# The order of the experts in a streamed mixture of experts: those of several items moved one distance forward

## The chip, the cores and the metric

The kernel runs on one core of one Trainium2 chip. The metric is device microseconds of one execution of the whole kernel. Three runs of the kernel before took 1101.43, 1099.33 and 1100.4 us; their median is 1100.4 us.

## The reference

One decoder layer is computed for 512 prompt tokens and for 32 sample tokens (8 sequences of 4): an input projection, an mLSTM branch and a sliding-window attention branch, their merge, a layer norm, a hierarchical mixture of experts with its layer norm, and a gated embedding with the last layer norm. The change lies in the mixture of experts alone:

```python
N_GROUPS, EXPERTS_PER_GROUP, TOP_K = 4, 8, 2        # 32 experts, D_MODEL 1024, D_EXPERT 512
def hier_moe(x, w_rg, b_rg, w_re, b_re, w_eg, w_eu, w_ed):
    g_idx = jnp.argmax(g_logits, axis=-1)                   # one group of experts for a token
    top_p, top_i = lax.top_k(softmax(e_logits_of_group), TOP_K)
    gate = g_w * top_p / top_p.sum(-1, keepdims=True)
    ...
def expert_block(args):
    h = jax.nn.silu(xblk @ w_gate[e]) * (xblk @ w_up[e])
    return h @ w_down[e]                                    # times gate, added to the token's row
```

Each of the 544 tokens goes to two experts. The sum over a token's two experts doesn't depend on the order in which the experts are worked off.

## The kernel before

**Items, places and slots.** After the router, the rows of each expert are cut into items of up to 32 rows. An expert has a place in a list; the program walks the list and, at each place, does all items of that expert. An expert's weights are 6 MB: gate and up in two halves of 2 MB each (tiles `w`, `w2a`, `w2b`, `gu3a`, `gu3b`) and down in two halves of 1 MB (`w`, `w2c`, `w2d`, `r_p`). There is room for four experts, slots 0 to 3 (NB = 4). Slots 0 and 1 have the tile name `w`, slot 2 has `w2a`, `w2b`, `w2c`, `w2d`, slot 3 has `gu3a`, `gu3b` and `r_p`. Place p uses slot p modulo 4, but the last places are put on the last slots: with 26 places, places 24 and 25 lie in slots 2 and 3, and so place 24 takes over the slot of place 22, and place 25 that of place 23 (the number `gap`, L219 to L225 and L395 to L412).

**The guess.** Four experts are fetched before the router has answered (L1749, `prefetch`). They are ranks 16 to 19 by the biases, and they stand at places 0 to 3 whatever the router says (`firsts`, L1808).

**The order of the others** is made by sorting keys on DVE (L2041 to L2080). An expert of one item (`kinds[:, 0]`) has the key n - 0.5, where n is its running number among those of one item, `nth[:, 0]`. An expert of several items (`kinds[:, 1]`) has the key n * ratio, where n is its running number among those of several, `nth[:, 1]`, and ratio is the number of those of one item divided by the number of those of several plus one (L2046 to L2050). `ties` adds a little for equal keys and puts the four fetched ahead in front; `base` adds 1000 where an expert has no item. So those of several items are spread evenly over those of one.

**The loads.** SP issues all weight loads in the order of the places (`load_place`, L199). Each load of place p waits for the place that had the slot before: for the first half of gate and up, until PE has done that half for its last item (semaphore `gh`), for the second half `gu`, and for the down weights `dn`, the last down product (L203 and L206). SP issues in order, so a load that waits holds back all loads behind it. Behind the last place's loads SP issues the `late` loads (L227): the rows x1 (2 MB) and the first half of `w_pg` (2 MB, semaphore `al`), which go into slot 0 and which the tail of the kernel needs.

**The work on an item.** PE does gate and up for the item (64 matmuls at L306 in the trace, 32 for each half), and then the down product of the item before (32 matmuls at L318 in the trace), since ACT (L440) and DVE (L515, L479) need time to turn gate and up into the hidden rows. DVE scales the product (L486) and POOL scatters it into `ybuf` (L265). Every fourth item PE transposes the next 128 rows (L298). The last item's down product stands at L415, its scaling at L533, its scatter at L286.

**The end of the stage.** It is one critical block: SP leaves it when all scatters have landed (L237 to L239) and ACT has finished (`fin`); ACT's last wait is for `al`, the landing of `w_pg` (L465). Only then does the tail begin (L2371 and on).

Of the kernel before, what the change touches and what calls it, by code (L numbers as in the profile page):

```python
# [15 lines left out]
ALU = mybir.AluOpType  # L16
# [528 lines left out]
def tile_decoder_step(ctx: ExitStack, tc: tile.TileContext, *aps):  # L545
    nc = tc.nc
    A = dict(zip(_INS + _CONSTS + _OUT_NAMES, aps))
    sy, act, dve, pe, gp = nc.sync, nc.scalar, nc.vector, nc.tensor, nc.gpsimd
# [125 lines left out]
    for pp in range(2):  # L674
        gp.dma_start(
            out=brow[16 + 4 * pp:20 + 4 * pp, :].rearrange("j (a d) -> j a d", a=2),
# [1260 lines left out]
    with ExitStack() as scope:  # L1937
# [26 lines left out]
        def rt(name, shape, dt=F32):  # L1964
            n = -(-count(shape) // 8) * 8
            if dt != F32 or taken[0] + n > arena.shape[1]:
                return R.tile(shape, dt, name=name)
            taken[0] += n
            return view(arena[:, taken[0] - n:taken[0] - n + count(shape)], shape)
# [21 lines left out]
        items, flag, base, key = (rt(n, [P, NEXP]) for n in ("items", "flag", "base", "key"))  # L1991
# [43 lines left out]
        kinds, nth = rt("kinds", [P, 2, NEXP]), rt("nth", [P, 2, NEXP])  # L2035
        ratio = rt("ratio", [P, 1])
# [12 lines left out]
        dve.scalar_tensor_tensor(out=key, in0=nth[:, 0], scalar=-0.5, in1=kinds[:, 0], op0=ALU.add, op1=ALU.mult)  # L2049
        dve.tensor_tensor(out=ratio, in0=ratio, in1=nth[:, 0, NEXP - 1:], op=ALU.mult)  # L2050
        dve.tensor_tensor(out=base, in0=base, in1=key, op=ALU.add)
        dve.scalar_tensor_tensor(out=key, in0=nth[:, 1], scalar=ratio, in1=kinds[:, 1], op0=ALU.mult, op1=ALU.mult)
        dve.tensor_tensor(out=key, in0=key, in1=base, op=ALU.add)

        E = NEXP
        sq, kcol, bcol_ = rt("sq", [E, E]), rt("kcol", [E, 1]), rt("bcol", [E, 1])
# [36 lines left out]
        for n, by, op, m_ in ((80, K["turns"][0:1], ALU.add, 16), (82, iota[0:1, 0:32], ALU.mult, 32)):  # L2093
# [4 lines left out]
                                 op0=ALU.mult, op1=ALU.subtract)  # L2098
# [10 lines left out]
                          in1=hi[:, :, None].to_broadcast([P, 2 * NT5, 20]), op=ALU.is_equal)  # L2109
# [357 lines left out]
```

## Time and profile before

| quantity | value |
|---|---|
| median of the runs | 1100.4 us |
| the profiled execution | 1102.54 us |
| its span, first to last instruction | 1100.6 us |
| PE busy | 1003.2 us (91%) |
| DVE busy | 512.0 us (47%) |
| ACT busy | 369.0 us (34%) |
| POOL busy | 255.7 us (23%) |
| bytes moved by DMA | 256.45 MB, 233 GB/s on the mean |

The busy shares are means over stages of different kinds. The stage of the experts runs from 646.84 us, PE's first matmul of place 0, to 1019.06 us, PE's first matmul of the tail. In the timeline PE's runs of matmuls at L306 carry the tile names of the slots, which gives the number of items at each place: 26 places with 49 items. Places 0 to 3 have one item each. The other 22 places, 4 to 25, have

1, 1, **2**, 1, **3**, 1, 1, **8**, 1, **3**, 1, 1, **3**, 1, **5**, 1, 1, **5**, 1, **2**, 1, 1

items: 14 places of one item, and 8 places of several (2, 3, 8, 3, 3, 5, 5, 2 in their order). All 26 experts are read once.

### The profile page before, as it was taken

What the parts mean: (1) busy time and instruction counts of PE and PEld (TensorE: products, weight loads), DVE (VectorE), ACT (ScalarE), POOL (GpSimd) and SP (SyncE); (2) the same over time, 40 slices, a digit from 0 to 9 for tenths busy, and PEclk for the clock granted to TensorE, in tenths of its full rate; (3) what the DMA queues carried; (4) which work ended last, traced back from release to release, by engine and by line L of the source; (5) the groups of instructions that cost most, each with busy time, mean ns of one, the idle gap of its engine ahead of it and who ended that gap; (6) DMA issues with size and microseconds to landing.
All of it is one profiled execution on the core that took longest, in us unless ns stands there. A gap on an engine that the chain in (4) does not pass through costs nothing.

```text
span 1100.6 us, 26984 instructions
## 1 busy us (share of the span) xinstructions
PE 1003.2 (91%) x10269; PEld 823.1 (75%) x10270; DVE 512.0 (47%) x1308; ACT 369.0 (34%) x751; POOL 255.7 (23%) x385
## 2 busy tenths in 40 slices
PE   9999999999999998999999976875988888986987
PEld 8988999999988886899989634553556565654775
DVE  5555533645767765565566731111122222222696
ACT  5311224533677776523321311110111111223531
POOL 6000000501355555312410211111222222221011
PEclk9999999999999998999999988999899999999699
DMA  8321322222515423534379889999999999979701
GB/s 257 78 78 54 101 77 77 67 68 85 159 46 184 156 97 122 183 93 137 109 278 407 339 307 393 426 427 426 426 427 426 427 426 427 426 319 400 291 34 63
DMA packets 90892, 256.45 MB, mean 233 GB/s; under 512 B 11115, under 2 KB 58433, under 8 KB 70820
## 3 DMA queue, kind: packets, MB, share of 16 engines
q1 hardware_dynamic: 76036, 224.61, 52.9%
q0 software_dynamic: 10272, 27.21, 7.0%
q10 hardware_dynamic: 4512, 3.64, 1.1%
q8 instruction: 49, 0.80, 0.3%
q14 instruction: 23, 0.19, 0.1%
HBM read 241.89 MB, written 19.61 MB: 238 GB/s over the span
## 4 chain that ended last, share of the span: by engine, by line
PE 77%; DMA 7%; issue 6%; SPq 4%; DVE 4%; ACT 1%; POOL 1%; DVEq 0%; ACTq 0%; POOLq 0%
PE pj L709 14%; PE pj L710 14%; PE pj L711 13%; PE psG L306 13%; PE kept L318 6%; SPq L137 3%; DMA gu3b<-in_w_eu_dram 2%; DMA w<-in_w_pg_dram 2%; SPq L143 1%; PE sp L1397 1%; PE psX L298 1%; PE nm L1385 1%; PE sp L767 1%; DMA wg_in<-in_w_in_dram 1%; PE pp L2267 1%
## 5 line engine op out<-in xcount | busy, mean ns | idle before, releaser
L709 PE MATMUL pj<-xH,wH 128*128 128x256 f32 (+1 forms) x672 | 197.4, 294 | 0.0
L710 PE MATMUL pj<-xL,wH 128*128 128x256 f32 (+1 forms) x672 | 196.1, 292 | 0.0
L711 PE MATMUL pj<-xH,wL 128*128 128x256 f32 (+1 forms) x672 | 194.7, 290 | 0.0
L592 ACT CAST wH<-raw 128x1024 fp32r<-128x1024 f32 x76 | 79.6, 1048 | 200.5 <-PE pj L710 127.1
L709 PEld LDWEIGHTS pj<-xH,wH 128*128 128x128 f32 x672 | 126.5, 188 | 4.6 <-issue 3.7
L710 PEld LDWEIGHTS pj<-xL,wH 128*128 128x128 f32 x672 | 126.4, 188 | 2.2 <-issue 1.6
L711 PEld LDWEIGHTS pj<-xH,wL 128*128 128x128 f32 x672 | 126.2, 188 | 2.1 <-issue 1.9
L593 DVE TENSOR_TENSOR wL<-raw,wH 128x1024 fp32r<-128x1024 f32 x76 | 95.4, 1256 | 64.7 <-ACT wH L592 64.5
L474 DVE COPY xT<-xg 128x256 f32 x48 | 14.4, 299 | 224.6 <-PE psG L306 224.6
L306 PE MATMUL psG<-w,xT 128*32 128x256 f32 x1408 | 87.0, 401 | 28.6 <-issue 23.2
L306 PEld LDWEIGHTS psG<-w,xT 128*32 128x32 f32 x1408 | 53.6, 115 | 60.0 <-issue 39.0
L440 ACT ACTIVATE both<-psG 128x128 f32<-128x128 f32 x49 | 13.6, 278 | 242.9 <-PE psG L306 242.9
L1373 POOL TENSOR_SCALAR lg<-lg,sm 128x256 f32<-128x256 f32 (+1 forms) x64 | 59.0, 934 | 44.9 <-DVE sm L1370 34.7
L265 POOL DMA_INDIRECT ybuf<-ysb,idy x48 | 47.6, 991 | 43.6 <-POOL idy L262 39.6
L426 ACT ACTIVATE xg<-psX,gcol 128x128 f32 (+1 forms) x100 | 36.3, 467 | 51.4 <-PE psX L298 51.4
L709 PE MATMUL pj<-wH,xH 128*128 128x256 f32 x160 | 46.8, 292 | 1.0 <-DVE vs L923 1.0
L318 PE MATMUL kept<-w,hT 128*32 128x256 f32 x704 | 44.2, 390 | 2.5 <-DVE hT L479 2.5
L710 PE MATMUL pj<-wL,xH 128*128 128x256 f32 x160 | 44.4, 277 | 0.0
L711 PE MATMUL pj<-wH,xL 128*128 128x256 f32 x160 | 44.3, 277 | 0.0
L306 PE MATMUL psG<-gu3a,xT 128*32 128x256 f32 x480 | 30.7, 398 | 14.7 <-issue 6.7
L479 DVE STREAM_TRANSPOSE hT<-both 128x128 f32<-128x128 f32 x49 | 20.1, 409 | 45.4 <-PE kept L318 45.0
L306 PE MATMUL psG<-w2a,xT 128*32 128x256 f32 x384 | 26.6, 423 | 15.9 <-issue 12.8
(655 smaller groups left out, 2281.4 us busy)
## 6 DMA issues: line engine op xcount, KB each, us to landing
w<-in_w_eg_dram SPq DMA_DIRECT2D x24, 1024.0 KB, 24.9
w<-in_w_eu_dram SPq DMA_DIRECT2D x24, 1024.0 KB, 27.2
w<-in_w_ed_dram SPq DMA_DIRECT2D x24, 1024.0 KB, 27.4
raw<-in_w_in_dram SPq DMA_DIRECT2D x22, 1024.0 KB
r_p<-in_w_ed_dram SPq DMA_DIRECT2D x14, 1024.0 KB, 24.5
w2a<-in_w_eg_dram SPq DMA_DIRECT2D x7, 1024.0 KB, 20.0
w2a<-in_w_eu_dram SPq DMA_DIRECT2D x7, 1024.0 KB, 22.4
w2b<-in_w_eg_dram SPq DMA_DIRECT2D x7, 1024.0 KB, 23.6
```

Source lines behind the costliest of these rows:

```text
L137: return [eng.dma_start(out=W[s][half][:, i], in_=w[i][bass.ds(e, 1)].rearrange("a (p k) f -> (a p) k f", p=P)[:, ks]) for i in range(2)]
L265: gp.indirect_dma_start(out=ybuf.rearrange("t (q d) -> (t q) d", q=4), out_offset=bass.IndirectOffsetOnAxis(ap=idy[:, r:r + 1], axis=0), i ...
L306: m = pe.matmul(psG[32 * q:32 * q + 32], xT[:, k], W[s][half][:, :, kh, P * q:P * q + P], start=k == 0, stop=k == KD - 1)
L318: m = pe.matmul(out[32 * q:32 * q + 32], hT[:, 32 * k:32 * k + 32], W[s][2][k // 2][:, k % 2, 256 * q:256 * q + 256], start=k == 0, stop=k ...
L426: m = act.activation(out=out, in_=psX[:, k], func=AF.Identity, bias=gcol[:, 1, k:k + 1], scale=gcol[:, 0, k:k + 1])
L479: dve.transpose(out=hT[:].rearrange("p (r t) -> p r t", r=4), in_=h[:].rearrange("p (f r) -> p r f", r=4)).then_inc(S["ch"], 1)
L592: act.copy(out=H, in_=src)
L593: return eng.tensor_tensor(out=L, in0=src, in1=H.bitcast(F32), op=ALU.subtract)
L709: pe.matmul(out, lh(k), rh(k), start=start and i == 0, stop=False)
L710: pe.matmul(out, lh(k), rl(k), start=False, stop=False)
L711: pe.matmul(out, ll(k), rh(k), start=False, stop=stop and i == len(ks) - 1)
L1373: gp.tensor_scalar(out=lg[:, par, j, 0:nk], in0=lg[:, par, j, 0:nk], scalar1=sm[:, 2, par, j:j + 1], scalar2=None, op0=ALU.mult)
```

## The change

Two DVE instructions that make the keys of the experts of several items:

```diff
-        dve.scalar_tensor_tensor(out=key, in0=nth[:, 1], scalar=ratio, in1=kinds[:, 1], op0=ALU.mult, op1=ALU.mult)
-        dve.tensor_tensor(out=key, in0=key, in1=base, op=ALU.add)
+        dve.scalar_tensor_tensor(out=key, in0=nth[:, 1], scalar=-1.0, in1=kinds[:, 1], op0=ALU.add, op1=ALU.mult)
+        dve.scalar_tensor_tensor(out=key, in0=key, scalar=ratio, in1=base, op0=ALU.mult, op1=ALU.add)
```

The key n * ratio becomes (n - 1) * ratio. The keys of the experts of one item, of the four fetched ahead and of those without items stay. With 14 of one item and 8 of several the ratio is 14/9 = 1.556: the keys of those of several were 1.556, 3.111, ... 12.444, and become 0, 1.556, ... 10.889, between those of one item at 0.5, 1.5, ... 13.5. Places 4 to 25 then have

**2**, 1, 1, **3**, 1, **8**, 1, 1, **3**, 1, **3**, 1, 1, **5**, 1, **5**, 1, 1, **2**, 1, 1, 1

items. The expert of eight items goes from place 11 to place 9, the last one of several (2 items) from place 23 to place 22. Slots, waits, the loads' order by place and the `late` loads are as before.

## Prediction

> **What bounds the kernel now.** I read the span first, then the windows over the stage of the experts, then PE's and SP's timelines there, and at last the chain that ended last. The first line is the page's span; the profiled execution took 1102.54 us, 1.94 above it and 2.1 above the runs' median of 1100.4. The sum below is made on this trace and carried to the median as a difference.
>
> ```profile
> span 1100.6 us, 26984 instructions
> ```
>
> The windows (length, busy PE, PEld, DVE, ACT, POOL, PEclk, DMA share, GB/s) show DMA at its ceiling for most of the stage, and one hole:
>
> ```profile
> 810.00:830.00 20.00, 16.14 (x293) 10.90 (x289) 4.25 (x13) 2.12 (x4) 3.64 (x7) 1.00 1.01 425
> 930.00:950.00 20.00, 16.98 (x264) 11.61 (x268) 2.78 (x8) 4.73 (x11) 4.79 (x8) 0.91 1.01 426
> ...
> 966.00:968.00 2.00, 2.00 (x44) 1.23 (x40) 0.00 (x0) 1.67 (x5) 1.02 (x2) 1.00 0.74 301
> 968.00:970.00 2.00, 1.83 (x36) 0.83 (x28) 0.52 (x3) 1.07 (x2) 1.22 (x2) 1.00 0.21 78
> 970.00:972.00 2.00, 0.60 (x12) 0.50 (x16) 0.85 (x2) 0.49 (x1) 1.17 (x2) 1.00 0.16 66
> 972.00:974.00 2.00, 2.00 (x44) 1.43 (x37) 0.00 (x0) 0.00 (x0) 0.98 (x1) 1.00 0.16 66
> 974.00:976.00 2.00, 2.00 (x44) 1.47 (x40) 0.49 (x2) 0.28 (x1) 0.00 (x0) 1.00 0.91 246
> ```
>
> Against 426 GB/s the five rows miss 125 + 348 + 360 + 360 + 180 = 1373, times 2 us, over 426: **6.45 us** of transfer are lost. SP's queue says why:
>
> ```profile
> 818.94 0.33 SPq L137 DMA_DIRECT2D gu3a<-in_w_eg_dram  x1
> ...
> 939.12 4.27 SPq L143 DMA_DIRECT2D r_p<-in_w_ed_dram  x2
> 973.53 0.34 SPq L137 DMA_DIRECT2D w2a<-in_w_eg_dram  x1
> ```
>
> Place 23's last load is issued at 939.12, place 24's first only at 973.53: slot 2 is still held by place 22. PE comes to place 22 late:
>
> ```profile
> 728.89 1.93 PE L306 MATMUL psG<-w,xT 128*32 128x256 f32 x32 [1.29 <-DMA w<-in_w_eu_dram]
> ...
> 747.10 3.66 PE L306 MATMUL psG<-w,xT 128*32 128x256 f32 x64 [2.03 <-issue]
> ...
> 760.50 1.93 PE L306 MATMUL psG<-w2b,xT 128*32 128x256 f32 x32 [1.39 <-DMA w2b<-in_w_eu_dram]
> ...
> 770.45 3.64 PE L306 MATMUL psG<-gu3a,xT 128*32 128x256 f32 x32 [6.29 <-DMA gu3a<-in_w_eu_dram]
> 775.20 3.64 PE L306 MATMUL psG<-gu3b,xT 128*32 128x256 f32 x32 [1.11 <-DMA gu3b<-in_w_eu_dram]
> 778.61 1.43 PE L318 MATMUL kept<-w2c,hT 128*32 128x256 f32 x16
> ...
> 787.66 1.93 PE L306 MATMUL psG<-gu3a,xT 128*32 128x256 f32 x32 [0.35 <-issue]
> ...
> 793.36 1.93 PE L306 MATMUL psG<-gu3a,xT 128*32 128x256 f32 x32 [0.31 <-issue]
> ...
> 851.16 1.93 PE L306 MATMUL psG<-w2a,xT 128*32 128x256 f32 x32 [1.52 <-issue]
> ...
> 858.06 1.93 PE L306 MATMUL psG<-gu3a,xT 128*32 128x256 f32 x32 [0.42 <-issue]
> ...
> 866.60 3.66 PE L306 MATMUL psG<-w,xT 128*32 128x256 f32 x64 [3.15 <-issue]
> ```
>
> Those are halves of the places 8, 9, 10, 11 (eight items), 14, 15 and 16. Up to place 11, PE waits for DMA. From 775.20 it has work without a break, since place 11 alone takes some 45 us, in which DMA fills the other slots. So PE is the late one from 775.20 to the hole. The next lines are place 22, place 23's two items and place 25's two halves:
>
> ```profile
> 971.40 1.93 PE L306 MATMUL psG<-w2a,xT 128*32 128x256 f32 x32 [1.56 <-issue]
> ...
> 978.04 1.93 PE L306 MATMUL psG<-gu3a,xT 128*32 128x256 f32 x32 [1.26 <-issue]
> ...
> 983.59 1.93 PE L306 MATMUL psG<-gu3a,xT 128*32 128x256 f32 x32 [0.16 <-issue]
> ...
> 999.60 1.93 PE L306 MATMUL psG<-gu3a,xT 128*32 128x256 f32 x32 [1.79 <-DVE both L515]
> 1002.21 1.93 PE L306 MATMUL psG<-gu3b,xT 128*32 128x256 f32 x32 [0.68 <-DMA gu3b<-in_w_eu_dram]
> ```
>
> Behind the hole DMA is the bound again: PE waits for place 25's gu3b, and the chain goes from SP's last issue through the landing of w_pg straight to the tail:
>
> ```profile
> 996.36 22.29 DMA w<-in_w_pg_dram
> 1018.65 0.02 issue
> ...
> 1019.06 3.75 PE po L150 x16
> ```
>
> So bytes that are late at 967 are late at 1018.65. All bytes are the same in both orders; only the hole can change.
>
> **The change, part by part.** *The two instructions.*
>
> ```profile
> L2052 DVE SCALAR_TENSOR_TENSOR xg<-nth,ratio,kinds x1: 253/253/253, 628.9 to 628.9; 128x32 f32<-128x32 f32 x1
> L2053 DVE TENSOR_TENSOR xg<-xg x1: 192/192/192, 629.2 to 629.2; 128x32 f32<-128x32 f32 x1
> ```
>
> The second becomes a scalar_tensor_tensor like the first, 192 to 253 ns: +0.06 us on the router's chain, counted in full (bounds 0 and +0.1).
>
> *Where PE's unbroken run begins.* The eight items now stand at place 9, slot 1. Places 4 to 8 hold eight items in five places in both orders (1, 1, 2, 1, 3 before; 2, 1, 1, 3, 1 after), so PE is through with them no later than before, at 747.10. The weights of place 9: the second halves of places 8 and 10 landed at 728.89 and 760.50, the middle is 744.7; by the step from place 10 to 11 (14.7) it is 745.8. I take 745, bounds 744.7 and 747.1. The run begins 30 us earlier.
>
> *When it reaches place 22.* Before, 971.40 - 775.20 = 196.2 us for 30 items at 11 places. After, there lie 32 items at 13 places between: two places of one item more. Such a place takes 858.06 - 851.16 = 6.9 us or 978.04 - 971.40 = 6.6 us, and 866.60 - 858.06 = 8.5 us where the loop turns over (bound). The same three turns and the same eight transposes lie between as before. 745 + 196.2 + 13.5 = 954.7; upper bound 747.1 + 196.2 + 17 = 960.3.
>
> *Place 24's first load.* Place 22 now has two items. The second follows the first by 793.36 - 787.66 = 5.7 us, its first half takes 1.93, SP issues 0.2 later (973.53 after 971.40 + 1.93): 962.5, bounds 962.2 and 968.1. It is needed before DMA runs dry. The 966 row's 301 GB/s put the last byte at 967.4; the 974 row's 246 puts the first new byte at 974.85, 1.3 after the issue. The deadline is 966.1: 3.6 us to spare, at the upper bound 2.0 us of hole.
>
> *What is late next.* SP then waits for place 22's last down product, behind place 23's gate and up: place 23 begins at 954.7 + 5.7 + 6.6 = 967.0, gate and up 3.66, down 1.9, so 972.6; place 24's gate and up, 4.19 MB at 426, keep DMA until 967.4 + 9.85 = 977.2. Place 25's loads queue behind and are not late either. The other new risk is place 13, which follows the eight items in slot 1 as place 15 did in slot 3. Place 15's load was issued 818.94 - 775.20 = 43.7 us after the run's begin, and the 810 row (425 GB/s) shows no hole there. Place 13's comes at 745 + 43.7 = 788.7; DMA has work to 745 + 4.9 (place 9's down, 2.1 MB at 426) + 3 x 15.8 (three places, each half of 760.50 - 728.89) = 797.3, so the deadline is 796.0.
>
> *The end.* w_pg lands 6.45 us earlier, at 1012.2. Beside it runs the last scatter:
>
> ```profile
> 1011.29 1.13 POOL L286 DMA_INDIRECT ybuf<-both,idy  x1 [1.90 <-DVE both L533]
> ...
> DMA to landing us min/median/max: 5.8/5.8/6.0
> ```
>
> It lands at 1011.29 + 5.8 = 1017.1, 14.9 after place 25's gu3b at 1002.21. That weight also lands 6.45 earlier, at 995.75, so the scatter at 1010.65 if PE runs as before. But PE will have had nothing to do for some 10 us between places 24 and 25: it is through with place 24's gate and up 3.66 after 977.2, and place 25's first half lands 4.9 before 995.75. After its 6.29 us of idleness at 770.45 both halves took 3.64 instead of 1.93, and the next sixteen matmuls 1.43: on place 25's second half that is 1.7, and some 0.4 behind it. The scatter lands at 1012.7, and now ends last, 0.5 behind w_pg.
>
> By the Trainium skill, "TensorE: Matmul & The Clock Gate", Part 1, an idle window of about 3.4 us halves PE's clock and as long a busy stretch restores it, and its advice to leave no such gaps speaks against singles at the end. By it, place 25's chain would lose half of 3.4, 1.7 us, and the stage would end at 1012.35. The trace agrees only roughly: 3.15 us idle before 866.60 left the 64 matmuls at 3.66.
>
> *The sum.* -6.45 (hole) + 0.5 (cold chain behind it) + 0.06 (key) = **-5.9 us**: the median goes to 1100.4 - 5.9 = 1094.5, the profiled execution to about 1096.6, its span to 1094.7.
>
> **The rivals.**
>
> *A: part of the hole stays*: PE comes to place 22 by 5 to 7.3 us later than summed (the upper bounds of its start and of the singles together are 5.6), which leaves a hole of 1.4 to 3.7: 1095.9 to 1098.2. For it: the margin of 3.6 us rests on a run of 210 us. Against: that run is a measured one plus two singles.
>
> *B: PE stays cold through the whole last chain*: gate, down, spread, down each lose about 1.7 (3.64 against 1.93 for 32 matmuls), 6.8 in all; the scatter lands at 1010.65 + 6.8 = 1017.5 and the gain is 1.15: 1099.3. For it: the stage's last three places are now single, with PE mostly idle. Against: at 778.61 PE was nearly warm again after 3.6 us. Here belongs, too, that the order comes out as before or that the hole was never on the path (1100.4); the keys and the chain speak against it.
>
> *C, slower: a hole behind the eight items.* Place: place 13's load. If PE's run at place 9 began x us after 745, for x over 7.3 there is a hole of x - 7.3 there, and the old hole at place 24 comes back with 3.7 besides (x - 3.6 less the first hole's x - 7.3). It decides from x = 12.3 on, where both exceed 6.45 by 2.2 us. At x = 15 it is 7.7 + 3.7 - 6.45 = 4.95: 1105.4. For it: three items at place 7 and eight at place 9 stand close together. Against: PE has done as many items by then as before, and was at place 9 at 747.10 then, and it had 6.29 us idle before place 11.
>
> **How the numbers follow.** Forecast 68%, A 13%, B and no change 12%, C 7%. Within 0.2%, 2.2 us, is about what a measurement of this kernel can't tell from no change (the runs lie 2.1 apart). Faster: 68 + 13 = 81%; same 12%; slower 7%. The predicted time is the likeliest case's, 1094.5, whose own range is 1092.9 (the whole hole gone, no cold chain, 1.05 of spread below) to 1096. Up to 1098.2 with A it holds 81%; I take B's 1099.3 in as the upper end, since the cold chain's length is the term with the fewest rows behind it.
>
> **What would show it.** In the windows: no row under 400 GB/s between 690 and 1005; in SP's queue, place 24's first w2a issue at 962 or before, with DMA still at 426; the eight items' run from about 745 to 790 in slot 1 (`w`), place 13's load at about 789; PE waiting for DMA at place 24 and at place 25; w_pg landing near 1012, the last scatter near it, the tail's first matmul near 1013; the tail itself, 81.5 us, unchanged. Wrong it would be if the hole stands at another place, if PE waits for nothing before place 24, or if the stage's end moves earlier and the tail grows.

## The result, and the profile after

The kernel after took 1093.27 us at the median (1091.31 to 1094.4, four runs), beside 1100.49 (1099.33 to 1101.43, four runs) for the kernel before on the same chip: a ratio of 0.993 [0.9906, 0.9955]. The forecast was 1094.5, faster, with 1092.9 to 1099.3 around it. The ratio puts 1100.4 at 1092.7 [1090.1, 1095.4]: the sign is right, the gain is 7.2 us by the medians where 5.9 were forecast, and the middle of the measurement lies 0.2 us under the low end. Two single executions of before, at 1417.9 and 1482.18 us, stand far outside all others and are left out of all that follows.

The profiled execution of after took 1093.82 us, 8.72 less than the 1102.54 of before. First its span:

```profile
span 1091.9 us, 26980 instructions
```

The windows of 2 us at the old hole, and one behind it (columns as before: busy PE, PEld, DVE, ACT, POOL, PEclk, DMA share, GB/s):

```profile
966.00:968.00 2.00, 2.00 (x44) 1.47 (x40) 0.38 (x1) 0.00 (x0) 0.56 (x2) 1.00 0.98 414
968.00:970.00 2.00, 2.00 (x44) 1.44 (x39) 0.49 (x2) 0.28 (x1) 0.61 (x1) 1.00 0.97 356
970.00:972.00 2.00, 0.66 (x15) 0.16 (x4) 0.88 (x2) 0.00 (x0) 0.00 (x0) 1.00 0.98 414
...
980.00:982.00 2.00, 1.45 (x28) 0.73 (x20) 0.00 (x0) 1.69 (x5) 0.91 (x1) 1.00 1.01 352
```

Where 78 and 66 GB/s stood, the lowest row has 356; behind it, the rows from 978 to 984 have 387, 352 and 360. DMA's share is 0.96 to 1.01 in all of these, so its engines had work and moved less. SP's queue in after: place 13's load, place 23's last, place 24's first, and w_pg:

```profile
789.54 0.33 SPq L137 DMA_DIRECT2D w<-in_w_eg_dram  x1
...
950.77 0.81 SPq L143 DMA_DIRECT2D r_p<-in_w_ed_dram  x2
967.41 0.34 SPq L137 DMA_DIRECT2D w2a<-in_w_eg_dram  x1
...
988.23 2.11 SPq L230 DMA_DIRECT2D w<-in_w_pg_dram  x1
```

Place 24's load goes out 6.1 us earlier than the 973.53 of before. PE's timeline has the eight items from 744.53, place 22 at 959.73, place 24 at 982.35, place 25's two halves, and the tail's first four groups:

```profile
744.53 5.35 PE L306 MATMUL psG<-w,xT 128*32 128x256 f32 x64 [2.17 <-issue]
...
809.57 5.35 PE L306 MATMUL psG<-w,xT 128*32 128x256 f32 x64 [3.08 <-issue]
...
865.37 5.27 PE L306 MATMUL psG<-w,xT 128*32 128x256 f32 x64 [3.12 <-issue]
...
943.65 5.35 PE L306 MATMUL psG<-w,xT 128*32 128x256 f32 x64 [3.19 <-issue]
...
959.73 1.93 PE L306 MATMUL psG<-w2a,xT 128*32 128x256 f32 x32 [1.39 <-issue]
...
982.35 1.93 PE L306 MATMUL psG<-w2a,xT 128*32 128x256 f32 x32 [0.90 <-issue]
...
992.89 3.64 PE L306 MATMUL psG<-gu3a,xT 128*32 128x256 f32 x32 [6.88 <-DMA gu3a<-in_w_eu_dram]
997.92 3.64 PE L306 MATMUL psG<-gu3b,xT 128*32 128x256 f32 x32 [1.39 <-DMA gu3b<-in_w_eu_dram]
...
1014.36 3.75 PE L150 MATMUL po<-gb,keep 48*128 48x128 f32 x16 [3.21 <-SPq L179]
1018.04 4.51 PE L2267 MATMUL pp<-keep 128*128 128x256 f32 x10
1022.48 2.05 PE L150 MATMUL po<-gb,keep 48*128 48x128 f32 x16
1024.45 1.99 PE L2267 MATMUL pp<-keep 128*128 128x256 f32 x8
```

The chain that ended last goes through place 25's second half and the last scatter, no longer through w_pg:

```profile
981.22 16.66 DMA gu3b<-in_w_eu_dram
997.92 3.64 PE psG L306 x32
...
1008.98 4.72 DMA ybuf<-both,idy
```

The stage ends 1019.06 - 1014.36 = 4.70 us earlier. The span is 8.7 shorter, so 4.0 came out of the tail (from PE's first matmul behind the stage to the end of the span), which the change doesn't touch. The same groups of before's tail show where:

```profile
1022.74 4.63 PE L2267 MATMUL pp<-keep 128*128 128x256 f32 x10
1027.31 3.78 PE L150 MATMUL po<-gb,keep 48*128 48x128 f32 x16
1031.02 3.78 PE L2267 MATMUL pp<-keep 128*128 128x256 f32 x8
```

The granted clock in before's windows there (PEclk, the third number from the end) is half to 1034, as in this row:

```profile
1029.00:1034.00 5.00, 5.00 (x17) 4.24 (x17) 1.52 (x3) 1.17 (x2) 0.00 (x0) 0.50 1.03 420
```

A spread (L150) is a group of matmuls of 48 rows by 128 columns, and its product (L2267) is the group behind it. The second spread and its product took 3.78 and 3.78 in before, and 2.05 and 1.99 in after: PE ran at half its clock for about 15 us at the tail's begin in the one profile, for about 8 us in the other. The four groups together are 3.6 of the 4.0 us. So two questions went to the chip: does the stage's gain come from the hole at place 24, and is the tail's part the change's work or chance?

### The profile page after: what moved, and what is told of

Read it like the earlier page. It is cut to its first block, busy times and chain, and to the rows that moved or that the text cites. A ratio compares the mean times of both kernels' runs of the same rounds, so it can differ in the third digit from the quotient of the medians.

```text
span 1091.9 us, 26980 instructions
## 1 busy us (share of the span) xinstructions
PE 1000.6 (92%) x10269; PEld 821.9 (75%) x10270; DVE 512.2 (47%) x1308; ACT 368.9 (34%) x751; POOL 255.8 (23%) x385
## 3 DMA queue, kind: packets, MB, share of 16 engines
q10 hardware_dynamic: 4512, 3.64, 1.1%
## 4 chain that ended last, share of the span: by engine, by line
PE 82%; issue 7%; DMA 5%; DVE 4%; ACT 1%; SPq 0%; POOL 0%; DVEq 0%; ACTq 0%; POOLq 0%
PE psG L306 17%; PE pj L709 14%; PE pj L710 14%; PE pj L711 14%; PE kept L318 7%; DMA gu3b<-in_w_eu_dram 2%; PE sp L1397 1%; PE psX L298 1%; PE nm L1385 1%; PE sp L767 1%; DMA w<-ybuf 1%; DMA wg_in<-in_w_in_dram 1%; PE po L711 1%; PE tp L1352 1%; PE tp L1350 1%
## 5 line engine op out<-in xcount | busy, mean ns | idle before, releaser
L306 PE MATMUL psG<-w,xT 128*32 128x256 f32 x1664 | 105.1, 408 | 28.6 <-issue 27.6
L306 PEld LDWEIGHTS psG<-w,xT 128*32 128x32 f32 x1664 | 64.0, 117 | 67.0 <-issue 44.6
L318 PE MATMUL kept<-w,hT 128*32 128x256 f32 x832 | 51.9, 388 | 2.5 <-DVE hT L479 2.5
L318 PEld LDWEIGHTS kept<-w,hT 128*32 128x32 f32 x832 | 31.9, 112 | 16.8 <-DVE hT L479 2.8
L306 PE MATMUL psG<-gu3a,xT 128*32 128x256 f32 x416 | 26.8, 400 | 15.4 <-issue 8.5
```

Source lines behind the costliest of these rows:

```text
L306: m = pe.matmul(psG[32 * q:32 * q + 32], xT[:, k], W[s][half][:, :, kh, P * q:P * q + P], start=k == 0, stop=k == KD - 1)
L318: m = pe.matmul(out[32 * q:32 * q + 32], hT[:, 32 * k:32 * k + 32], W[s][2][k // 2][:, k % 2, 256 * q:256 * q + 256], start=k == 0, stop=k ...
```

## The experiments

Theories for the stage. **T1**, the prediction's: the time lies in the hole, which goes because PE's long run begins earlier and so place 22 is done, and place 24 loaded, earlier. **T2**: the gain comes from the end of the order, where the last places are now single items and little work is left for PE behind the last bytes. For the tail: either the length of PE's idle time ahead of it sets how long it runs cold (theory C), or it is chance, and differs between executions of one kernel.

All kernels keep the computation; where matmuls are added, their results are not used. Each ratio is to runs of before on the same chip.

**Front alone.** All experts of several items but the last move forward; the last stays where it was in before. From place 4 on: 2, 1, 1, 3, 1, 8, 1, 1, 3, 1, 3, 1, 1, 5, 1, 5, 1, 1, 1, 2, 1, 1 items. Against after:

```diff
-        dve.scalar_tensor_tensor(out=key, in0=nth[:, 1], scalar=-1.0, in1=kinds[:, 1], op0=ALU.add, op1=ALU.mult)
+        dve.scalar_tensor_tensor(out=flag, in0=nth[:, 1], scalar=nth[:, 1, NEXP - 1:], in1=nth[:, 1], op0=ALU.is_ge, op1=ALU.add)
+        dve.scalar_tensor_tensor(out=key, in0=flag, scalar=-1.0, in1=kinds[:, 1], op0=ALU.add, op1=ALU.mult)
```

> The seven other experts of several items move one distance forward, the last one (2 items) stays at place 23. Theory 1 (the unbroken run of PE begins earlier, so place 22 is done before DMA runs dry): place 22 is a single, place 24's first load is issued 5.6 us before the changed kernel's 967.4, near 962; no hole; the stage ends as in the changed kernel, the tail's first matmul near 1014; about 1093. Theory 2 (the gain comes from what stands last, three singles instead of a pair and two singles): as before, 1100.5, with a hole of about 6 us.

Measured: 1092.38 us (1089.99 to 1094.94), ratio 0.9922 [0.9896, 0.9949]. Place 24's first load and the tail's begin in its profile:

```profile
961.34 0.34 SPq L137 DMA_DIRECT2D w2a<-in_w_eg_dram  x1
...
1013.44 3.75 PE L150 MATMUL po<-gb,keep 48*128 48x128 f32 x16 [2.96 <-SPq L179]
```

The whole gain is there with before's end of the order (place 23 with two items). T2 falls.

**End alone.** Only the last of several moves, against before; places 4 to 20 stay, the last have 5, 2, 1, 1, 1:

```diff
-        dve.scalar_tensor_tensor(out=key, in0=nth[:, 1], scalar=ratio, in1=kinds[:, 1], op0=ALU.mult, op1=ALU.mult)
-        dve.tensor_tensor(out=key, in0=key, in1=base, op=ALU.add)
+        dve.scalar_tensor_tensor(out=flag, in0=nth[:, 1], scalar=nth[:, 1, NEXP - 1:], in1=nth[:, 1], op0=ALU.is_ge, op1=ALU.subtract)
+        dve.scalar_tensor_tensor(out=key, in0=flag, scalar=ratio, in1=kinds[:, 1], op0=ALU.mult, op1=ALU.mult)
+        dve.tensor_tensor(out=key, in0=base, in1=key, op=ALU.subtract)
```

> Only the last expert of several items moves, from place 23 to 22; the eight items stay at place 11. Theory 1: place 24's first load waits for place 22's second item, 973.5 + 5.6 = 979.1; the hole grows from 6.45 to about 12 us and the time by 5.6, to 1106. Theory 2: the last three places are single as in the changed kernel, so most of the stage's gain is there: about 1095.

Measured: 1107.61 us (1106.05 to 1112.02), ratio 1.0058 [1.0029, 1.0086]. Place 22 has two items now and is no earlier, so the slot is held longer:

```profile
981.05 1.93 PE L306 MATMUL psG<-w2a,xT 128*32 128x256 f32 x32 [0.16 <-issue]
```

```profile
970.00:972.00 2.00, 2.00 (x44) 1.17 (x36) 0.00 (x0) 1.78 (x6) 1.12 (x2) 1.00 0.43 158
972.00:974.00 2.00, 1.93 (x36) 0.91 (x28) 0.49 (x2) 0.97 (x2) 1.22 (x2) 1.00 0.06 16
...
980.00:982.00 2.00, 1.84 (x39) 1.06 (x32) 0.75 (x2) 0.00 (x0) 0.00 (x0) 1.00 0.00 0
```

The first row is the first half of place 22's second item at 981.05; place 24's load followed at 983.18. The rows below are windows in the hole, which is about twice as long. Half of the change by itself makes the kernel slower: with two items place 22 holds its slot for longer, and nothing ahead of it has moved forward to make up for that. (In this profile the whole stage also begins 2.2 us later than in the mean of before's, at 649.32, which is part of its late end.)

**Half the distance, and half a distance too late.** In after's line the constant -1.0 becomes -0.5 (the eight items at place 10), or +1.0 (the eight at place 12, five at place 22, two at the last place):

```diff
-        dve.scalar_tensor_tensor(out=key, in0=nth[:, 1], scalar=-1.0, in1=kinds[:, 1], op0=ALU.add, op1=ALU.mult)
+        dve.scalar_tensor_tensor(out=key, in0=nth[:, 1], scalar=-0.5, in1=kinds[:, 1], op0=ALU.add, op1=ALU.mult)
```

> Half a distance forward: eight items at place 10, pair still at place 23. Theory 1: the run begins 14.7 us earlier than before and has one single (6.7 us) more to do, place 22 begins about 963.4 to 967, place 24's first load 965.5 to 969: a hole of 0 to 3 us, the tail's first matmul near 1014 to 1016. Theory 2: as before, hole about 6 us, 1019.

> One distance backward: eight items at place 12, five items at place 22, the pair last. Theory 1: the run begins 15.8 us later than before, place 22's fifth item is at about 980, place 24's first load at about 982: a hole of about 15 us, and two items instead of one behind the last weights, 5.6 us more: about 1114. Theory 2: only the pair at the end counts: about 1106.

Measured: half the distance 1092.57 us (1091.09 to 1096.9), ratio 0.9935 [0.9908, 0.9962], place 24's load at 965.35; later 1107.61 us (1104.41 to 1112.03), ratio 1.0069 [1.0036, 1.0102], place 24's load at 977.73. The order can be moved both ways, and the time follows the hole at place 24's load. (End alone and the later order come to the same time although their loads went out 5 us apart: DMA ran dry at about 969 in the one and at about 965 in the other.) Once the load is early enough, nothing more is won: half the distance gives what the whole one gives. The later order was expected at 1114 and came to 1107.61. Its load went out at 977.73 and not at 982, and the hole cost 13.4 us and not 15; that is a part of the 6 us, and the rest isn't split up.

**The two kernels again, unchanged**, for the tail and for the spread:

> The kernel before, unchanged: a second profile of its tail. Theory C (the clock at the tail's start follows from how long PE sat idle ahead of it, 5.5 us before and 3.2 us after): the tail takes 81.5 us again, with PE at half clock for some 15 us. Theory P (it is chance where the clock's window falls): the tail may as well take 77.5 us, with half clock for some 8 us.

> The changed kernel, unchanged. Theory C: the tail takes 77.5 us again. Theory P: it may take 77 to 82 us.

> The kernel before, a third profile. What is open is how often its tail takes 81.5 us (first profile) or 76.8 (second). If the long tail is chance (theory P): the stage ends at 1017 to 1019 with a hole of 6.5 to 7 us, and the tail takes 76.5 to 78 or about 81.5. If the order before brings it about: about 81.5 in most profiles.

> As the third: hole 6.5 to 7 us, stage's end 1017 to 1019, tail either 76.5 to 78 or about 81.5.

> The changed kernel, a third profile. Theory P: no hole over 2 us, the stage ends at 1013 to 1014.5, and the tail may be long (about 81.5) here as well as short. If the order decides: short.

Measured: before 1096.63 us (1092.01 to 1101.8, ten runs; ratio to the other runs of before there 0.9986 [0.9962, 1.001]), after 1093.49 us (1088.82 to 1094.96, eleven runs), ratio 0.995 [0.993, 0.997]. Three more profiled executions, one each, took 1099.32 and 1099.25 us for before and 1092.76 for after. The tail in the second profile of before:

```profile
1017.44 3.75 PE L150 MATMUL po<-gb,keep 48*128 48x128 f32 x16 [5.80 <-SPq L179]
1021.12 3.75 PE L2267 MATMUL pp<-keep 128*128 128x256 f32 x10
1024.79 2.05 PE L150 MATMUL po<-gb,keep 48*128 48x128 f32 x16
1026.77 1.99 PE L2267 MATMUL pp<-keep 128*128 128x256 f32 x8
```

5.80 us of idle time ahead, the longest of all profiles, and a short tail: theory C falls. Before's long tail was one of four, and none of the nine other profiles in the table has one. All profiles together (loss: the shortfall of the 2 us windows from 960 to 1000 against 426 GB/s, as time; stage end: PE's first matmul of the tail; tail: the span less that):

| kernel | span | place 24's load | loss | stage end | tail |
|---|---|---|---|---|---|
| before | 1100.6 | 973.53 | 6.96 | 1019.06 | 81.5 |
| before, second | 1094.2 | 972.18 | 6.89 | 1017.44 | 76.8 |
| before, third | 1097.4 | 973.62 | 7.72 | 1019.21 | 78.2 |
| before, fourth | 1097.3 | 974.38 | 9.06 | 1019.65 | 77.7 |
| after | 1091.9 | 967.41 | 1.44 | 1014.36 | 77.5 |
| after, second | 1091.6 | 963.82 | 0.26 | 1013.51 | 78.1 |
| after, third | 1090.9 | 966.98 | 1.33 | 1012.66 | 78.2 |
| front alone | 1091.1 | 961.34 | 0.24 | 1013.44 | 77.7 |
| end alone | 1104.9 | 983.18 | 14.06 | 1028.22 | 76.7 |
| half the distance | 1090.7 | 965.35 | 0.62 | 1012.81 | 77.9 |
| later | 1104.9 | 977.73 | 13.39 | 1027.97 | 76.9 |
| before, filled | 1095.8 | 971.83 | 7.67 | 1019.41 | 76.4 |
| after, filled | 1091.0 | 966.45 | 1.93 | 1014.58 | 76.4 |

Means of the four of before and the three of after: loss 7.66 and 1.01 (-6.65), stage end 1018.84 and 1013.51 (-5.33), tail 78.5 and 78.0 (-0.6, from the unrounded values), span 1097.4 and 1091.5 (**-5.9**). The stage begins between 646.3 and 648.0 in all rows but end alone; at the mean it begins 0.5 us later in after than in before.

**Matmuls put ahead of the tail.** Behind PE's last wait of the stage, eight products of 128 by 256 in before, four in after (16 and 8 in the trace), to keep PE warm:

```diff
         pe.wait_ge(S["sc"], len(halves))
+        for _ in range(8):
+            pe.matmul(wide[0][:, 0:256], ident, any_, start=True, stop=True)
```

> The order before, with 8 matmuls more on PE (128x256 f32, results unused) between the last copies of the stage and its end, so that PE isn't idle there. The stage ends as before, 1019. If the slow clock at the tail's start is what the tail's 4 us hang on, it starts warm: the tail takes 77.5 us or less and the time is 1096.5. If the tail's 4 us hang on something else (when DMA brings ybuf's rows, say), it stays 81.5 and 1100.5.

> The changed order, with 4 such matmuls at the same place. In the changed kernel's profile PE was done with the tail's first matmuls before the rows were normalised, so a warm start is worth at most 1 us there: 1092 to 1093.3; where a run of the changed kernel has the long cold tail, up to 4 us.

Measured: before filled 1100.83 us (1095.28 to 1103.45), ratio 1.002 [0.9997, 1.0043]; after filled 1093.64 us (1090.27 to 1095.22), ratio 0.9955 [0.9937, 0.9973], no better than after beside it. In before's:

```profile
1012.35 6.74 PE L419 MATMUL psX<-keep 128*128 128x256 f32 x16 [0.68 <-ACT r_p L457]
...
1019.41 2.02 PE L150 MATMUL po<-gb,keep 48*128 48x128 f32 x16 [0.32 <-SPq L179]
```

The added matmuls ran cold themselves, 6.74 us for 16, but behind them the tail's first spread took 2.02 instead of 3.75. The tail is 76.4 in both, about 2 less than the 78.5 and 78.0 of the means. The timed runs show none of these 2 us in either kernel; where they go in the executions without a profile stays open.

**A warm last chain.** Eleven products ahead of place 25's items, in the loop over the slots:

```diff
+                if s == NB - 1:
+                    with pe.If(a + 1 > full):
+                        pe.wait_ge(S["c4"], ng)
+                        for _ in range(11):
+                            pe.matmul(wide[0][:, 0:256], ident, any_, start=True, stop=True)
```

> The changed order, with 11 matmuls more on PE (128x256 f32, results unused) between place 24's and place 25's gate and up, so that PE is not idle there. If the cold chain behind place 25's weights sets the stage's end: both halves of place 25 take 1.93 instead of 3.64, the last scatter lands 1.5 to 2 us earlier, and the stage ends where w_pg lands, 0.3 to 0.7 us earlier than in the first profile of the changed kernel. If the cold chain is hidden: no change within 0.2 us.

Measured: 1191.84 us (1187.81 to 1194.5), ratio 1.0847 [1.0825, 1.0868]. The edit changed something else as well. PE's groups behind a turn of its loop over the places, here the first of them, and the chain's rows:

```profile
704.76 6.19 PE L306 MATMUL psG<-w,xT 128*32 128x256 f32 x64 [17.79 <-issue]
```

```profile
846.37 18.42 issue
...
1018.55 13.78 issue
```

The same turn in after:

```profile
687.75 5.34 PE L306 MATMUL psG<-w,xT 128*32 128x256 f32 x64 [3.55 <-issue]
```

What DMA carried for instructions in the stage (packets, MB, share), first this kernel's from 650 to 1110, then after's from 650 to 1010:

```profile
q8 instruction: 53, 0.87, 0.8%
```

```profile
q8 instruction: 6, 0.10, 0.1%
```

47 more packets of instructions, and 13.8 to 18.4 us without work ahead of the first group behind each of the five turns instead of 2.4 to 3.6. Together that is 81 us instead of 15, some 66 of the 98 us that this kernel is slower than after; the rest isn't split up. The rows speak for PE's loop being fetched again at each turn once its body is that little longer. That is argued from the rows, not tried by itself. On the cold chain the run says nothing; the profiles of after answer that, below.

## Where the prediction was right, and which step failed

**The mechanism in the stage is shown.** The hole at place 24 was worth nearly what the stage's end moved: 6.65 us of loss went, the stage ended 5.33 earlier and had begun 0.5 later, and the cold chain at the end, below, took some tenths back. Front alone takes the hole away and keeps the gain (loss 0.24, 1092.38 us), end alone doubles it and is slower by about 6.4 us (0.0058 of 1100.8), and in the table the kernels with a loss of 13 to 14 end the stage at 1028, those with 7 to 9 at 1017 to 1020, those under 2 at 1013 to 1015. The forecast's -5.9 is the difference of the mean spans. That the figures are equal is luck in part, since the spans of before's four profiles lie 6.4 apart. The runs agree in kind: 72 of before (1092.0 to 1105.7) have the median 1098.8, 16 of after (1088.8 to 1095.0) have 1093.1. But these are mixed from several chips. On the chip of the first runs the medians differ by 7.2 us; on the chip of the repeats, with 43 and 11 runs, by 3.9 (the means by 5.4). So the gain is sure, and its size is known to about 2 us.

**Where the run begins** was right: 744.53 against 745. **When it reaches place 22** was not: 959.73 against 954.7, 5.0 later, under the bound of 960.3. The run takes 215.2 us instead of the 209.7 summed. Four groups of 64 matmuls in after took 5.3 us instead of 3.66, at the run's begin and behind 3.1 to 3.2 us of idle time where the loop turns over: 1.7 each. Before's run held two such losses, the second half at 775.20 and one turn:

```profile
931.83 5.35 PE L306 MATMUL psG<-w,xT 128*32 128x256 f32 x64 [3.11 <-issue]
```

Two more make 3.4 of the 5.5; the other 2.1 lie within the bounds of the two singles (13.5 to 17). The second profile of after begins warm, has two cold groups (at 808.22 and 940.06), and comes to place 22 that much earlier:

```profile
744.96 3.66 PE L306 MATMUL psG<-w,xT 128*32 128x256 f32 x64 [1.96 <-issue]
...
940.06 5.35 PE L306 MATMUL psG<-w,xT 128*32 128x256 f32 x64 [3.25 <-issue]
...
956.10 1.93 PE L306 MATMUL psG<-w2a,xT 128*32 128x256 f32 x32 [1.38 <-issue]
```

**Place 24's first load** therefore came at 967.41, not 962.5, past the deadline of 966.1, and some loss stayed: 1.44, against 0.26 in the second profile. Only 0.44 of it stands at the old hole (the rows from 966 to 972), and 0.84 from 978 to 984; since DMA's share is near 1 in these rows, they speak for slower transfers rather than missing work, and why they are slower isn't shown. So the condition of rival A (5 us late) just came true, but not its price: a hole of 1.4 at place 24 didn't come. The prediction's "no row under 400 GB/s" failed with 356 and 352. And one of its signs of being wrong appeared: PE did not wait for DMA ahead of place 24 in this profile (0.90 on issue), since it came there late itself. In the second profile, with two cold groups less, it did wait, for place 24's second half:

```profile
982.62 1.93 PE L306 MATMUL psG<-w2b,xT 128*32 128x256 f32 x32 [1.83 <-DMA w2b<-in_w_eu_dram]
```

**What is late next** was right. Place 13's load went out at 789.54 (forecast 788.7), and no hole came:

```profile
790.00:810.00 20.00, 13.96 (x253) 9.05 (x249) 4.13 (x12) 2.71 (x6) 4.60 (x8) 1.00 1.01 426
```

So rival C, the slower one, had no place to act. **The end** was right in kind: place 25 waits for both its halves, both took 3.64, and from gu3b's start to the last scatter's there are now 1008.98 - 997.92 = 11.06 us, where before had 1011.29 - 1002.21 = 9.08: 2.0 for the cold chain, forecast 2.1. The scatter lands at 1008.98 + 4.72 = 1013.70, w_pg at 988.23 + 25.3 = 1013.5. In the second profile of after the second half ran warm, and w_pg ended last:

```profile
997.65 1.93 PE L306 MATMUL psG<-gu3b,xT 128*32 128x256 f32 x32 [1.82 <-DMA gu3b<-in_w_eu_dram]
```

```profile
987.96 25.15 DMA w<-in_w_pg_dram
```

It lands at 1013.11, and its stage ends at 1013.51. A chain that is cold or warm thus decides only 0.2 to 0.6 us here; rival B, cold all the way down, didn't come.

**The step that failed** is the tail: "the tail itself, 81.5 us, unchanged", and with it the "1.05 of spread below" that set the low end of the range. The prediction took 81.5 from one profile as fixed, and its spread from three runs that lay 2.1 us apart. In the first pair of profiles the tail moved by 4.0 us where nothing was forecast, and the stage by 4.70 where 5.9 were. The repeats show what the 81.5 was: the tails of before's four profiles are 81.5, 76.8, 78.2 and 77.7. PE's clock came back after 6 to 9 us in three of them and after 15 in one, and the first profile held that one. They don't show that the change won anything in the tail: the means are 78.5 and 78.0, and without the long one before's is 77.6. The runs of before lie 11.6 us apart on one chip (43 runs, 1092.0 to 1103.6), more than five times the 2.1 that the prediction had. The 4.7 us between the four tails and the 2.2 between the four losses are part of that; the rest isn't traced. The 16 runs of after lie between 1088.8 and 1095.0, and the forecast's low end, 1092.9, stands inside them: it allowed for the hole and the cold chain, and hardly for the runs' own spread. How much of the 7.2 us between the first medians came out of the tail isn't known, since only one execution of each kernel there has a trace.

## What to carry to other kernels

When weights stream through a ring of slots, ask how early the compute engine's long run of work begins: here that set the lead of the transfers at the end, and half of the move was as good as all of it. Move an order as a whole: here, moving only the last pair one place forward held a slot for longer and lost time. One distribution of items was measured; with another the hole may stand elsewhere. Before a stage that was not touched is credited with a gain, the unchanged kernel wants a second profile.

## What the runs showed of the hardware

**Idle times of 2 to 3 us halve PE's clock, sometimes.** 2.17 us ahead of 744.53 and 3.08 ahead of 809.57 in after cost 1.7 us each; 3.15 ahead of 866.60 in before cost nothing. The same group behind the same gap was warm in the first profile of before and cold in the fourth:

```profile
825.44 3.66 PE L306 MATMUL psG<-w,xT 128*32 128x256 f32 x64 [3.24 <-issue]
```

```profile
822.10 5.35 PE L306 MATMUL psG<-w,xT 128*32 128x256 f32 x64 [3.23 <-issue]
```

The Trainium skill, "TensorE: Matmul & The Clock Gate", Part 1, describes a free-running window of about 3.4 us, and one idle window as what halves the clock. A gap that is cold in one execution and warm in the next fits a window that runs free; that gaps of 2.17 and 3.08 us are enough does not fit its length, and there the measurement decides.

**Spreads of 48 rows did not bring the clock back.** The tail's first spread kept PE busy for 3.75 us at half clock, and the matmuls of 128 rows behind it were cold still (4.63, 4.51 or 3.75 us). The matmuls put ahead of the tail ran cold too, though they followed 3.88 us of such spreads at once (6.74 us for 16), and after them PE was warm. Those spreads did not hold the clock either: in the filled profile of before it was 1.00 in the windows from 1006 to 1010 and 0.50 from 1012 on, and PE had been idle for 0.68 us between. Whether it is the rows or the moment isn't shown.

**A loop's turn on PE left it 2.4 to 3.6 us without work in after, and 13.8 to 18.4 us with the body a little longer**, in the kernel with the eleven products: one condition, one wait and eleven matmuls in the loop, and about 98 us more for the kernel. That the instructions' fetching is the reason is argued from the packets, not shown.
